# Two-block transformer layer on one core: the upper feed-forward matrices of the second block by seven products of quarters instead of eight

## The chip, the cores and the metric

The kernel runs on one core of a Trainium2 chip. The metric is device time in microseconds (us) of one execution of the whole program, on that core; lower is better. The kernel before took 3178.87 us, the median of three runs (3176.96, 3178.87 and 3190.85).

## The reference, cut to what matters

Two blocks run one after the other on 512 tokens of 1024 features. The first has four sequence mixers and a mixture of 32 experts. The second has two layers of the same shape, and the change is in the feed-forward half of these two:

```python
def hybrid_layer(h, ..., w1, w3, w2, ln2_g, ln2_b, cos, sin):
    ...
    h = layer_norm(ALPHA * h + mix, ln1_g, ln1_b)
    a = jnp.einsum('bld,df->blf', h, w1)
    b = jnp.einsum('bld,df->blf', h, w3)
    y = jnp.einsum('blf,fd->bld', jax.nn.silu(a) * b, w2)
    return layer_norm(ALPHA * h + y, ln2_g, ln2_b)
```

Here `h` has 528 tokens in the first layer (16 of them meta tokens) and 512 that matter in the second; `w1` and `w3` ("upper" matrices) are 1024 x 2816, which is 22 tiles of 128 hidden features each, and `w2` is 2816 x 1024. All is float32.

## The kernel before, in words

**Arithmetic.** A float32 product is made of float32r products. Each operand is cut exactly into a high part `h` (a copy rounded to float32r, on ACT) and a low part `l` (operand minus high part), and three matmuls are summed: high by high, high by low, low by high (`mmf_steps`, L1771 to L1778, with the matmuls on L1775 to L1777). Activations lie feature-major, so the weights are the stationary operand and the tokens the moving one. The tokens go in two halves, of 264 in the first layer and 256 in the second.

**One hidden tile.** A weight tile is a piece of 128 x 1024 (eight blocks of 128 input features). For a hidden tile `f` and a half of the tokens, each of the two matrices takes 8 x 3 matmuls into one PSUM bank. So one hidden tile takes 2 matrices x 2 halves x 24 = 96 matmuls. Then ACT takes the silu of the first product (L2274), Vector multiplies by the second (L2275), and when both halves are there ACT and POOL split the result (L2283, L2284) for the lower product.

**Stages of a layer.** `ffn_ln` (L2255) goes through three parts of the hidden features (`FPARTS`: 8, 8 and 6 tiles). After each part's upper products come the lower products with `w2` (8 output tiles; matmuls on L2297 to L2299), summed into `r`. The first two hidden tiles are treated together: both tiles' first token half, then both tiles' second half, because the second half of `h1` is still being normalised; `rest()` is the end of that norm.

**Weights.** `Split` (L1108) streams all pieces of the second block in order of use through a ring of six slots of 128 x 2048. A slot holds two raw pieces, loaded on SP's queue (512 KB each), or the two parts of one piece, made by ACT (L1141) and Vector (L1142).

**Order.** The program is written stage by stage, and a scheduler then fixes the order on each engine when the program is built; each engine runs its own list strictly in that order. PSUM has eight banks: six for products ("gu" four, "py" two, handed out in turn by `bank`), two for small things.

Of the kernel before, what the change touches and what calls it, by code (L numbers as in the profile page):

```python
# [32 lines left out]
FT = [  # name, columns (-1: zero)  # L33
# [93 lines left out]
def layout(inp):  # L127
    """The inputs laid out for the loads: transposed, cut and padded with zeros."""
# [59 lines left out]
    # experts, in units in the order of use: half, gate or linear, k half; k half, half  # L188
# [10 lines left out]
# ---- second block: 16 meta tokens and 512 tokens, 528 in all  # L199
# [45 lines left out]
def _ret_tables():  # L245
    """rotary tables with the decay gamma^(t - 264) (q) and gamma^(264 - t) / sqrt(dk) (k) folded in"""
# [19 lines left out]
def layout2(inp, o):  # L266
# [57 lines left out]
# ---------------------------------------------------------------- device  # L324
# [30 lines left out]
def softplus_steps(k, pool, z, out):  # L355
    """out = softplus(z) = max(z, 0) + log1p(exp(-|z|))"""
# [17 lines left out]
def block1_mix(k, es_mix):  # L374
    """In-projection and the four mixers. Returns their outputs side by side, feature-major
    [128, 8, 512], in two float32r parts, in a pool of es_mix."""
    nc, tc, A = k.nc, k.tc, k.A
    V, ACT, G, PE = nc.vector, nc.scalar, nc.gpsimd, nc.tensor
    with ExitStack() as es:
# [28 lines left out]
        def wt(shape, name, bufs=1):  # L408
            """working tile; the larger ones share slots by size"""
# [44 lines left out]
        def tproj(name, evac):  # L454
            """one token tile at each step"""
# [24 lines left out]
        def tgate(name):  # L480
            """u * sigmoid(u)"""
# [21 lines left out]
        def conv(name, cw, cb, j, out):  # L503
            """out = silu(causal conv of width 4)"""
# [11 lines left out]
        # ---- row quantities: dt and the cumulated decay (SSD), gates (mLSTM)  # L516
# [75 lines left out]
        # ---- SSD  # L592
        def ssd():
# [61 lines left out]
        # ---- GLA  # L655
        def gla():
# [15 lines left out]
            sc = wt([128, NCH], "gl_sc")     # state: end of chunk c to the middle of c+1  # L672
# [55 lines left out]
        # ---- mLSTM  # L728
        def mlstm():
# [11 lines left out]
            # the gate as tanh(u / 2) = 2 sigmoid(u) - 1  # L741
# [48 lines left out]
        # ---- the mixers' outputs and the weights of the output projection, two float32r parts each  # L790
# [8 lines left out]
        def out_piece(n, i):  # L799
            """two blocks of rows of half n of the columns"""  # L800
# [6 lines left out]
        # ---- RWKV: everything but the recurrence over chunks  # L807
# [97 lines left out]
        def rwkv_chunks():  # L905
# [40 lines left out]
            def bank4(l):  # L946
                """psum for one half of the columns of four heads"""
# [106 lines left out]
# the slots of a block of an expert's tokens, and room for the table of the further blocks  # L1054
# [4 lines left out]
def rsqrt(k, pool, v, out, scale=1.0, eps=0.0):  # L1059
    """out = (v * scale + eps) ** -0.5 for narrow v [p, m]: Newton's iterations from a guess by the exponent"""  # L1060
# [20 lines left out]
def fast_rsqrt(k, pool, v, out, scale=1.0, eps=0.0):  # L1081
    """the same with the tables of logarithm and exponential, where they are loaded"""
# [1423 lines left out]
```

## Time and profile before

| what | value |
|---|---|
| runs | 3176.96, 3178.87, 3190.85 us; median 3178.87 |
| profiled execution | span 3183.1 us from the first to the last instruction; the page gives no other time of it |
| TensorE (PE) busy | 3025.6 us, 95% |
| VectorE (DVE) busy | 2144.0 us, 67% |
| ScalarE (ACT) busy | 1533.5 us, 48% |
| GpSimd (POOL) busy | 819.9 us, 26% |
| mean granted TensorE clock | 0.965 of full speed |

A slice of the span can be bound by another engine than the next slice, so these shares are only a start: the feed-forward stages of the second block are the last third of the span, and have to be read by themselves. "Busy" of PE counts pipelined matmuls, whose recorded lengths overlap; how fast PE goes is read from how many matmuls start in a stretch. An instruction's recorded length also overlaps the next one's start a little on DVE, so the distance between starts tells more than the length.

### The profile page before, as it was taken

To read this page: it belongs to the slowest core of one execution; us is meant where nothing else is said; L and a number is where in the kernel's file an instruction comes from. 1 tells how busy PE (TensorE), PEld (TensorE's weight loads), DVE (VectorE), ACT (ScalarE), POOL (GpSimd) and SP (SyncE) were. 2 spreads that over 40 slices of the span, in tenths; PEclk is the share of its full clock that TensorE was granted. 3 is DMA by queue.
4 is the path that set the end of the run, shared out by engine and by line. 5 is a ranking of instruction groups with operands and counts; after the bars stand their busy time and mean duration, and the time that the engine had idled before them with its cause. 6 is when DMAs were issued, how large, how long until landed. Compare 5 with 4: busy or idle time off the path is not lost. (4 is left out here: it accounts for less than half of the span.)

```text
span 3183.1 us, 45711 instructions
## 1 busy us (share of the span) xinstructions
PE 3025.6 (95%) x18347; PEld 2488.6 (78%) x18347; DVE 2144.0 (67%) x3036; ACT 1533.5 (48%) x1840; POOL 819.9 (26%) x538
## 2 busy tenths in 40 slices
PE   6899879999999999999999899999999899999997
PEld 4799666666666666666666788999999899999997
DVE  4745758999999989799988766653333846834324
ACT  4411426677766666676666644342222534432222
POOL 1210233333333333234322320320102501410104
PEclk8989889999999999999999989999999889999998
DMA  3201268999999999799997121122222211222221
GB/s 121 73 21 41 85 255 319 340 348 350 351 353 340 343 343 334 300 351 344 343 343 244 51 91 41 65 82 91 84 93 80 95 45 50 80 97 90 97 85 52
DMA packets 105991, 581.58 MB, mean 183 GB/s; under 512 B 13016, under 2 KB 13544, under 8 KB 55792
## 3 DMA queue, kind: packets, MB, share of 16 engines
q1 hardware_dynamic: 94784, 540.86, 45.9%
q0 software_dynamic: 10896, 37.52, 4.4%
q8 instruction: 145, 2.38, 0.3%
q14 instruction: 70, 0.57, 0.1%
q10 hardware_dynamic: 96, 0.26, 0.0%
HBM read 559.64 MB, written 18.94 MB: 182 GB/s over the span
## 5 line engine op out<-in xcount | busy, mean ns | idle before, releaser
L1211 DVE TENSOR_TENSOR wl<-w,wh 128x2048 fp32r<-128x2048 f32 (+1 forms) x398 | 909.3, 2293 | 85.0 <-ACT wh L1210 84.0
L1210 ACT ACTIVATE wh<-w 128x2048 fp32r<-128x2048 f32 (+1 forms) x410 | 734.1, 1808 | 133.2 <-PE gu L1150 87.1
L1775 PE MATMUL gu<-hh,w 128*128 128x256 f32 (+2 forms) x1552 | 454.6, 293 | 8.3 <-ACT hh L2473 8.3
L1776 PE MATMUL gu<-hl,w 128*128 128x256 f32 (+2 forms) x1552 | 451.3, 291 | 3.5 <-DVE hl L2475 2.7
L1777 PE MATMUL gu<-hh,w 128*128 128x256 f32 (+2 forms) x1552 | 449.1, 290 | 0.8 <-DVE w L1142 0.8
L1149 PE MATMUL gu<-wl,xT 128*96 128x512 f32 x1024 | 414.6, 405 | 8.8 <-DVE wl L1211 7.4
L1148 PE MATMUL gu<-wh,xT 128*96 128x512 f32 x1024 | 406.1, 397 | 0.2 <-ACT wh L1210 0.2
L1150 PE MATMUL gu<-wh,xT 128*96 128x512 f32 x1024 | 403.9, 394 | 0.0
L1142 DVE TENSOR_TENSOR w<-w 128x1024 fp32r<-128x1024 f32 (+1 forms) x190 | 237.6, 1251 | 234.1 <-ACT w L1141 229.8
L1141 ACT ACTIVATE w<-w 128x1024 fp32r<-128x1024 f32 (+1 forms) x194 | 201.2, 1038 | 259.5 <-PE gu L2299 84.6
L1775 PEld LDWEIGHTS gu<-hh,w 128*128 128x128 f32 x1552 | 300.6, 194 | 11.0 <-ACT hh L2473 9.9
L1776 PEld LDWEIGHTS gu<-hl,w 128*128 128x128 f32 x1552 | 300.0, 193 | 6.6 <-DVE hl L2475 4.4
L1777 PEld LDWEIGHTS gu<-hh,w 128*128 128x128 f32 x1552 | 300.9, 194 | 2.0 <-DVE w L1142 1.3
L1424 POOL TENSOR_TENSOR hg<-hg,sg 96x512 f32<-96x512 f32 x64 | 171.5, 2680 | 333.7 <-ACT sg L1422 333.7
L1149 PEld LDWEIGHTS gu<-wl,xT 128*96 128x96 f32 x1024 | 165.3, 161 | 106.6 <-DVE wl L1211 33.2
L2284 POOL TENSOR_TENSOR al<-fs,ah 128x528 fp32r<-128x528 f32 (+1 forms) x44 | 76.7, 1744 | 608.1 <-ACT ah L2283 608.1
L1148 PEld LDWEIGHTS gu<-wh,xT 128*96 128x96 f32 x1024 | 165.9, 162 | 73.4 <-issue 1.9
L1150 PEld LDWEIGHTS gu<-wh,xT 128*96 128x96 f32 x1024 | 165.8, 162 | 62.6
L1149 PE MATMUL py<-wl,hT 128*96 128x512 f32 x512 | 206.5, 403 | 0.2
L1148 PE MATMUL py<-wh,hT 128*96 128x512 f32 x512 | 204.3, 399 | 0.1
L1150 PE MATMUL py<-wh,hT 128*96 128x512 f32 x512 | 200.9, 397 | 0.0
L1444 POOL DMA_INDIRECT h_d<-y,dx x31 | 119.1, 3840 | 226.2 <-ACT y L1443 222.2
(701 smaller groups left out, 6478.0 us busy)
## 6 DMA issues: line engine op xcount, KB each, us to landing
w<-in_wgu SPq DMA_DIRECT2D x255, 1024.0 KB, 7.3
w<-in_wdn SPq DMA_DIRECT2D x127, 1024.0 KB, 6.5
w<-in_w SPq DMA_DIRECT2D x88, 512.0 KB, 3.5
w<-in_w2f SPq DMA_DIRECT2D x43, 512.0 KB, 3.7
w<-in_w22a SPq DMA_DIRECT2D x32, 512.0 KB, 3.8
w<-in_w1f SPq DMA_DIRECT2D x18, 512.0 KB, 3.5
w<-in_w2o SPq DMA_DIRECT2D x16, 512.0 KB, 3.6
w<-in_w22b SPq DMA_DIRECT2D x16, 384.0 KB, 3.4
```

Source lines behind the costliest of these rows:

```text
L1141: nc.scalar.activation(h, w, AF.Copy)
L1142: (eng or nc.vector).tensor_sub(l, w, h.bitcast(F32))
L1148: PE.matmul(out, a[0], b[0], start=start, stop=False)
L1149: PE.matmul(out, a[0], b[1], start=False, stop=False)
L1150: PE.matmul(out, a[1], b[0], start=False, stop=stop)
L1210: ACT.activation(h[:, j], w[:, j], AF.Copy)
L1211: (early or V).tensor_sub(l[:, j], w[:, j], h[:, j].bitcast(F32))
L1424: G.tensor_mul(hg, hg, sg)
L1444: G.indirect_dma_start(out=h_d, out_offset=bass.IndirectOffsetOnAxis(ap=dx[:, :1], axis=0), in_=y, in_offset=None, compute_op=OP.add)
L1775: PE.matmul(p, w[0][:, kk], x[0][:, kk, c], start=kk == ks[0], stop=False)
L1776: PE.matmul(p, w[0][:, kk], x[1][:, kk, c], start=False, stop=False)
L1777: PE.matmul(p, w[1][:, kk], x[0][:, kk, c], start=False, stop=kk == ks[-1])
```

## The change

Two hidden tiles of one upper matrix and the two halves of the tokens make a product of 2 x 2 quarters: the hidden tiles `f` and `f+1`, the upper and lower four blocks of input features, and the two token halves. Eight products of quarters are needed when written out plainly. The change computes the same with seven (Strassen's algorithm in Winograd's form), each of them 4 blocks x 3 matmuls = 12 into one bank. It needs sums of weight quarters, sums of token quarters, and sums of the seven products:

- `Split.pair` makes seven stationary operands of 128 x 512 from two raw pieces: three subtractions on POOL, one addition on Vector, and seven splits, each a copy on ACT and a subtraction on Vector. The parts fill three slots of the ring and a tile `sp_p` (two buffers).
- `token_sums` makes the four sums of token quarters once per layer, in place in `r`, and splits them.
- `seven` runs the seven products and combines them: one ACT copy and seven Vector additions from PSUM, then `done` for each finished quarter: silu on ACT for `w1`, a multiplication on POOL for `w3`.
- The first two hidden tiles of each layer stay as they were, but one after the other; the other 20 go in ten pairs, for both matrices: 20 pairs of weight tiles per layer, 40 in all.
- Around it: the pieces' order (w1 of both tiles, then w3 of both), buffers of `ah`/`al` (8 for 10), `fs` (4 for 2), the norm's `ln_s`, `ln_T`, `ln_Q` (1 for 2), a bias written back into `r` after the first norm (an ACT instruction for each even tile), the lookahead `AHEAD` set at places, and the last norm's tiles in a pool of their own.

```diff
 class Split:
+    def pair(self, src0, src1, pool):
+        ...
+        w0, w1 = self.raw.pop(0), self.raw.pop(0)
+        a11, a12, a21, a22 = w0[:, 0:512], w0[:, 512:1024], w1[:, 0:512], w1[:, 512:1024]
+        room = []
+        for _ in range(3):
+            t = self.slot(F32R)
+            room += [(t[:, 1024 * i:1024 * i + 512], t[:, 1024 * i + 512:1024 * i + 1024]) for i in range(2)]
+        t = pool.tile([128, 1024], F32R, name="sp_p", bufs=2)
+        room.append((t[:, 0:512], t[:, 512:1024]))
+        t1, t2 = (pool.tile([128, 512], F32, name=n) for n in ("sp_a", "sp_b"))
+
+        def parts(i, x):
+            h, l = room[i]
+            ACT.activation(h, x, AF.Copy)
+            V.tensor_sub(l, x, h.bitcast(F32))
+
+        parts(0, a11)
+        V.tensor_add(t1, a21, a22)
+        G.tensor_sub(t2, t1, a11)
+        parts(1, t2)
+        parts(2, a12)
+        G.tensor_sub(a21, a11, a21)
+        parts(3, a21)
+        parts(4, t1)
+        G.tensor_sub(t2, a12, t2)
+        parts(5, t2)
+        parts(6, a22)
+        return [[x.rearrange("p (a b) -> p a b", a=4) for x in r] for r in room]
...
+    def seven(self, w, h1, T, t0, hn, room, done, bank):
+        def product(i, x, kh, c):
+            p = bank()
+            for kk in range(4):
+                for a, b in ((0, 0), (0, 1), (1, 0)):
+                    PE.matmul(p, w[i][a][:, kk], x[b][:, kh + kk, c], start=kk == a == b == 0, stop=kk == 3 and a == 1)
+            return p
+        ...
+        ACT.activation(r11, product(0, h1, 0, c0), AF.Copy)
+        V.tensor_add(r12, r11, product(1, T[1], 0, ct))
+        V.tensor_add(r11, r11, product(2, h1, 4, c0))
+        done(0, 0)
+        V.tensor_add(r21, r12, product(3, T[2], 0, ct))
+        p = product(4, T[0], 0, ct)
+        V.tensor_add(r22, r21, p)
+        V.tensor_add(r12, r12, p)
+        done(1, 1)
+        V.tensor_add(r12, r12, product(5, h1, 4, c1))
+        done(0, 1)
+        V.tensor_add(r21, r21, product(6, T[3], 0, ct))
+        done(1, 0)
+
+    def token_sums(self, r, pool, hn):
+        ...
+        V.tensor_sub(t[0], b[0][1], b[0][0])
+        G.tensor_sub(t[2], b[1][1], b[0][1])
+        V.tensor_sub(t[1], b[1][1], t[0])
+        V.tensor_sub(t[3], b[1][0], t[1])
+        for i in range(4):
+            ACT.activation(T[i][0], t[i], AF.Copy)
+            V.tensor_sub(T[i][1], t[i], T[i][0].bitcast(F32))
+        return T
...
     def ffn_ln(...):
-                for fs in [(f0, f0 + 1)] * (i == 0) + [(f,) for f in range(f0 + 2 * (i == 0), f1)]:
-                    ws = {(f, nm): self.piece(A[nm][l, f]) for f in fs for nm in ("w21", "w23")}
-                    ...
-                            ACT.activation(ss[f][:, c], pu, AF.Silu)
-                            V.tensor_mul(ss[f][:, c], ss[f][:, c], pg)
+                for f in range(2) if i == 0 else []:
+                    ...
+                        if rest:
+                            rest()
+                            T, rest = self.token_sums(r, tp, hn), None
+                    out(ss)
+                for f in range(f0 + 2 * (i == 0), f1, 2):
+                    s2 = [fs_(), fs_()]
+                    quarter = {(a, b): s2[a][:, half[b]] for a in range(2) for b in range(2)}
+                    def silu(a, b):
+                        ACT.activation(quarter[a, b], quarter[a, b], AF.Silu)
+                    self.seven(sp.pair(A["w21"][l, f], A["w21"][l, f + 1], ff), h1, T, t0, hn, quarter, silu, pt)
+                    tmp = {(a, b): ff.tile([128, hn], F32, name="fg%d%d" % (a, b)) for a in range(2) for b in range(2)}
+                    def times(a, b):
+                        G.tensor_mul(quarter[a, b], quarter[a, b], tmp[a, b])
+                    self.seven(sp.pair(A["w23"][l, f], A["w23"][l, f + 1], ff), h1, T, t0, hn, tmp, times, pt)
+                    for s_ in s2:
+                        out(s_)
```

**Vector in the second part of the first layer.** In the rows below L1142 splits a whole piece before, L1172 a quarter now; L1175 is the weight sum; L2275 is the multiplication before; L2313 to L2323 are the additions of the products from PSUM ("gu" and "py"). `w_19909` is the raw slot of a w3 pair, `w_19912` to `w_19914` and `sp_p_19915` its parts, `fg..` the products of the w3 pair two places ahead of it in the program, `fs_19773` those of the w1 pair between the two. Before, for two hidden tiles:

```order
L2275 TENSOR_TENSOR fs_17921<-fs_17921,gu_17923 128x264
L1142 TENSOR_TENSOR w_18151<-w_18030,w_18151 128x1024
L2275 TENSOR_TENSOR fs_17921<-fs_17921,py_17975 128x264
L1142 TENSOR_TENSOR w_18154<-w_18030,w_18154 128x1024
L2275 TENSOR_TENSOR fs_18039<-fs_18039,gu_18041 128x264
L1142 TENSOR_TENSOR w_18269<-w_18148,w_18269 128x1024
```

Now, for one pair of weight tiles (its last split, of `sp_b`, comes next):

```order
L1172 TENSOR_TENSOR w_19912<-w_19909,w_19912 128x512
L2318 TENSOR_TENSOR fg11_19634<-fg10_19633,gu_19719 128x264
L2319 TENSOR_TENSOR fg01_19632<-fg01_19632,gu_19719 128x264
L1175 TENSOR_TENSOR sp_a_19916<-w_19909 128x512
L2321 TENSOR_TENSOR fg01_19632<-fg01_19632,py_19735 128x264
L1172 TENSOR_TENSOR w_19913<-w_19909,w_19913 128x512
L1172 TENSOR_TENSOR w_19912<-sp_b_19917,w_19912 128x512
L2323 TENSOR_TENSOR fg10_19633<-fg10_19633,gu_19750 128x264
L1172 TENSOR_TENSOR w_19913<-w_19909,w_19913 128x512
L1172 TENSOR_TENSOR sp_p_19915<-w_19909,sp_p_19915 128x512
L1172 TENSOR_TENSOR w_19914<-sp_a_19916,w_19914 128x512
L2313 TENSOR_TENSOR fs_19773<-fs_19773,py_19816 128x264
```

Two splits for two products have become eight instructions on weights among seven additions of products, and the additions of one pair stand behind the splits of the pair after next.

**POOL at the same place.** Before, one low part for each hidden tile:

```order
L2284 TENSOR_TENSOR al_17905<-fs_17646,ah_17904 128x528
L2284 TENSOR_TENSOR al_17909<-fs_17647,ah_17908 128x528
L2284 TENSOR_TENSOR al_18027<-fs_17921,ah_18026 128x528
L2284 TENSOR_TENSOR al_18145<-fs_18039,ah_18144 128x528
L2284 TENSOR_TENSOR al_18263<-fs_18157,ah_18262 128x528
```

Now, for two hidden tiles (L1176, L1179 and L1182 are the weight subtractions, L2392 the multiplications, L2362 the low parts):

```order
L1176 TENSOR_TENSOR sp_b_20057<-sp_a_20056,w_20049 128x512
L1179 TENSOR_TENSOR w_20049<-w_20049 128x512
L1182 TENSOR_TENSOR sp_b_20057<-w_20049,sp_b_20057 128x512
L2392 TENSOR_TENSOR fs_19773<-fs_19773,fg00_19905 128x264
L2392 TENSOR_TENSOR fs_19774<-fs_19774,fg11_19908 128x264
L1176 TENSOR_TENSOR sp_b_20191<-sp_a_20190,w_20183 128x512
L2392 TENSOR_TENSOR fs_19773<-fs_19773,fg01_19906 128x264
L1179 TENSOR_TENSOR w_20183<-w_20183 128x512
L2362 TENSOR_TENSOR al_20040<-fs_19773,ah_20039 128x528
L1182 TENSOR_TENSOR sp_b_20191<-w_20183,sp_b_20191 128x512
L2392 TENSOR_TENSOR fs_19774<-fs_19774,fg10_19907 128x264
L2362 TENSOR_TENSOR al_20044<-fs_19774,ah_20043 128x528
```

Two instructions for two hidden tiles have become twelve, for two pairs of weight tiles.

**PE at the start of the first layer's feed-forward.** Here `w_17631` and `w_17634` are w1 and w3 of hidden tile 0, `w_17640` and `w_17643` those of tile 1 before; `w_17633` and `w_17636` are those of tile 0 now. Before, where the second half of the tokens begins:

```order
L1777 MATMUL gu_17701<-hh_17039,w_17643 128x264
L1775 MATMUL gu_17800<-hh_17039,w_17631 128x264
L1775 MATMUL py_17801<-hh_17039,w_17634 128x264
L1775 MATMUL gu_17852<-hh_17039,w_17640 128x264
L1775 MATMUL gu_17853<-hh_17039,w_17643 128x264
L1776 MATMUL gu_17800<-hl_17040,w_17631 128x264
```

Now, where it begins:

```order
L1819 MATMUL gu_17641<-hh_17039,w_17636 128x264
L1817 MATMUL py_17764<-hh_17039,w_17633 128x264
L1817 MATMUL gu_17765<-hh_17039,w_17636 128x264
L1818 MATMUL py_17764<-hl_17040,w_17633 128x264
L1819 MATMUL py_17764<-hh_17039,w_17633 128x264
```

Tile 1's 48 matmuls with the first half stood ahead of this point before; now only tile 0's do, and tile 1's come later.

## Rows read from the trace of the kernel before

**Rows 1.** The page's busy times: us, share of the span, instructions.
```profile
PE 3025.6 (95%) x18347; PEld 2488.6 (78%) x18347; DVE 2144.0 (67%) x3036; ACT 1533.5 (48%) x1840; POOL 819.9 (26%) x538
```

**Rows 2.** Busy us and counts by window: PE, PEld, DVE, ACT, POOL; clock, DMA, GB/s.
```profile
2270.91:2329.27 58.36, 58.36 (x482) 58.36 (x481) 16.54 (x21) 16.62 (x25) 8.82 (x5) 1.00 0.25 91
2806.19:2862.99 56.80, 56.80 (x482) 56.80 (x481) 16.47 (x20) 16.49 (x25) 9.04 (x5) 1.00 0.26 93
```

**Rows 3.** Time line of DVE, one hidden tile of layer two: start, length, instruction.
```profile
2800.58 0.42 DVE L2275 TENSOR_TENSOR fs<-fs,gu 128x256 f32<-128x256 f32 x1 [3.43 <-PE gu L1777]
2804.71 1.22 DVE L1142 TENSOR_TENSOR w<-w 128x1024 fp32r<-128x1024 f32 x1 [3.71 <-ACT w L1141]
...
2807.33 1.23 DVE L1142 TENSOR_TENSOR w<-w 128x1024 fp32r<-128x1024 f32 x1 [0.72 <-ACT w L1141]
2811.94 0.42 DVE L2275 TENSOR_TENSOR fs<-fs,gu 128x256 f32<-128x256 f32 x1 [3.38 <-PE gu L1777]
```

**Rows 4.** Time line of DVE, instructions back to back while POOL is idle.
```profile
2740.72 0.68 DVE L2442 TENSOR_TENSOR ln_Q<-ln_Q,ln_sq 128x512 f32<-128x512 f32 x1
2741.33 0.68 DVE L2240 SCALAR_TENSOR_TENSOR r<-hl,r 128x512 f32<-128x512 f32 x1
2741.93 0.41 DVE L2430 TENSOR_TENSOR r<-r,gu 128x256 f32<-128x256 f32 x1
2742.26 1.21 DVE L1142 TENSOR_TENSOR w<-w 128x1024 fp32r<-128x1024 f32 x1
```

**Rows 5.** Groups by line: count, busy us, mean ns of one, idle before.
```profile
L1210 ACT ACTIVATE wh<-w 128x512 fp32r<-128x512 f32 x12 | 6.6, 619 | 0.5 <-PE gu L1150 0.5
...
L2284 POOL TENSOR_TENSOR al<-fs,ah 128x528 fp32r<-128x528 f32 x22 | 38.6, 1755 | 308.9 <-ACT ah L2283 308.9
...
L2478 POOL TENSOR_TENSOR r<-r,ln_T 128x264 f32<-128x264 f32 x16 | 15.1, 970 | 9.2 <-ACT ln_T L2455 9.2
```

**Rows 6.** Time lines of POOL and DVE where both work, at three places.
```profile
2496.91 3.54 POOL L2477 TENSOR_TENSOR r<-r,ln_mean 128x264 f32<-128x264 f32 x4 [4.48 <-ACT ln_mean L2451]
...
2496.68 0.48 DVE L2471 SCALAR_TENSOR_TENSOR r<-ln_mrs,cp,r 128x264 f32<-128x264 f32 x1
2497.08 0.97 DVE L2475 SCALAR_TENSOR_TENSOR hl<-r,cp,hh 128x264 fp32r<-128x264 f32 x1
2497.97 0.97 DVE L2470 SCALAR_TENSOR_TENSOR r<-r,cp,ln_T 128x264 f32<-128x264 f32 x1
...
2730.93 3.44 POOL L2426 TENSOR_TENSOR r<-r,ln_s 128x512 f32<-128x512 f32 x2 [1.74 <-issue]
...
2733.14 1.78 DVE L2240 SCALAR_TENSOR_TENSOR r<-hl,r 128x512 f32<-128x512 f32 x1
...
2487.92 4.12 POOL L2478 TENSOR_TENSOR r<-r,ln_T 128x264 f32<-128x264 f32 x4 [0.77 <-ACT ln_T L2455]
...
2490.45 0.41 DVE L2430 TENSOR_TENSOR r<-r,py 128x264 f32<-128x264 f32 x1
```

**Rows 7.** Landing times of the loads on L1126 (SP).
```profile
DMA to landing us min/median/max: 2.9/3.6/5.9
```

**Rows 8.** Start of layer one's feed-forward: windows as in rows 2, PE, DVE.
```profile
2095.00:2101.00 6.00, 4.11 (x34) 3.90 (x32) 4.11 (x7) 4.65 (x7) 3.52 (x4) 1.00 0.44 165
2101.00:2107.00 6.00, 4.70 (x25) 4.48 (x26) 5.42 (x14) 4.40 (x11) 0.09 (x1) 0.72 0.01 3
...
2101.22 0.39 PE L1775 MATMUL gu<-hh,w 128*128 128x264 f32 x1 [2.10 <-ACT hh L2473]
...
2097.36 0.43 DVE L2456 SCALAR_TENSOR_TENSOR ln_mrs<-ln_mean,ln_T 128x264 f32<-128x264 f32 x1 [1.89 <-ACT ln_T L2455]
...
2106.23 0.42 DVE L1684 TENSOR_TENSOR hl<-r,hh 128x264 fp32r<-128x264 f32 x1
```

More of the change, by code (lines that the diff above doesn't have):

```diff
@@ L1143, in __call__ @@
         return h, l
+    def pair(self, src0, src1, pool):
+        nc = self.k.nc
+        V, ACT, G = nc.vector, nc.scalar, nc.gpsimd
+        for i, src in enumerate((src0, src1)):
+            want = self.srcs[self.n + i]
+            assert (want.tensor.name, want.offset, want.shape) == (src.tensor.name, src.offset, src.shape)
+        while self.loaded < self.n + 2:
+            self.load()
+        self.n += 2
+        w0, w1 = self.raw.pop(0), self.raw.pop(0)
[23 more added lines that the diff above has]
+        return [[x.rearrange("p (a b) -> p a b", a=4) for x in r] for r in room]
 def mm3(PE, out, a, b, start, stop):
@@ L1714, in run @@
                     hp = ExitStack()
-                    last = l == k.n_layers - 1
-                    h = None if last else self.new_h(hp, "right")
-                    self.ffn_ln(l, h1, h, t0, LayerNorm(self, lp, r, T2 - t0, "ln2", l, t0), rest)
+                    new = None if l == k.n_layers - 1 else lambda: self.new_h(hp, "right")
+                    h = self.ffn_ln(l, h1, new, t0, LayerNorm(self, lp, r, T2 - t0, "ln2", l, t0), rest)
                 h1p.close()
@@ L1729, in pieces @@
         for i, (f0, f1) in enumerate(FPARTS):
-            for f in range(f0, f1):
-                yield A["w21"][l, f]
-                yield A["w23"][l, f]
+            for f in range(f0, f1, 2):
+                for j in ((f, "w21"), (f, "w23"), (f + 1, "w21"), (f + 1, "w23")) if f == 0 else \
+                        ((f, "w21"), (f + 1, "w21"), (f, "w23"), (f + 1, "w23")):
+                    yield A[j[1]][l, j[0]]
             for m in range(8):
@@ L2253, in proj_ln, with ffn_ln @@
         return self.late(3, tile, mm, ln, h1)
-    def ffn_ln(self, l, h1, hn_, t0, ln, rest):
+    def seven(self, w, h1, T, t0, hn, room, done, bank):
+        PE, V, ACT = self.nc.tensor, self.nc.vector, self.nc.scalar
+        def product(i, x, kh, c):
[4 more added lines that the diff above has]
+            return p
+        c0, c1, ct = slice(t0, t0 + hn), slice(t0 + hn, t0 + 2 * hn), slice(0, hn)
+        r11, r12, r21, r22 = (room[ab] for ab in ((0, 0), (0, 1), (1, 0), (1, 1)))
+        ACT.activation(r11, product(0, h1, 0, c0), AF.Copy)
[12 more added lines that the diff above has]
+    def token_sums(self, r, pool, hn):
+        nc = self.nc
+        V, ACT, G = nc.vector, nc.scalar, nc.gpsimd
+        b = [[r[:, 4 * i:4 * i + 4, hn * j:hn * j + hn] for j in range(2)] for i in range(2)]
+        T = [[pool.tile([128, 4, hn], F32R, name="T%d%d" % (i, j)) for j in range(2)] for i in range(4)]
+        t = [b[0][0], b[1][1], b[0][1], b[1][0]]
+        V.tensor_sub(t[0], b[0][1], b[0][0])
[6 more added lines that the diff above has]
+        return T
+    def ffn_ln(self, l, h1, new, t0, ln, rest):
         nc, A, sp = self.nc, self.A, self.sp
@@ L2261, in ffn_ln, with out @@
         r, pt = ln.r, ln.bank
+        half = [slice(0, hn), slice(hn, n)]
         with tile_pool(self.tc, name="ff", bufs=1) as ff:
+            es_t = ExitStack()
+            tp = es_t.enter_context(tile_pool(self.tc, name="ts", bufs=1, side="right"))
             for i, (f0, f1) in enumerate(FPARTS):
                 act = []
[L2265 to L2275 removed]
+                def out(s_):
+                    a = (ff.tile([128, n], F32R, name="ah", tag="ah", bufs=8),
+                         ff.tile([128, n], F32R, name="al", tag="al", bufs=8))
+                    ACT.activation(a[0], s_, AF.Copy)
+                    G.tensor_sub(a[1], s_, a[0].bitcast(F32))
+                    act.append(a)
+                fs_ = lambda: ff.tile([128, n], F32, name="fs", bufs=4)
+                for f in range(2) if i == 0 else []:
+                    sp.AHEAD = 2 - f
+                    ws = {nm: self.piece(A[nm][l, f]) for nm in ("w21", "w23")}
+                    ss = fs_()
+                    for q in range(2):
+                        pu, pg = pt(), pt()
+                        for nm, p in (("w21", pu), ("w23", pg)):
+                            self.mmf(p, ws[nm], h1, range(8), slice(t0 + hn * q, t0 + hn * q + hn))
+                        ACT.activation(ss[:, half[q]], pu, AF.Silu)
+                        V.tensor_mul(ss[:, half[q]], ss[:, half[q]], pg)
                         if rest:
@@ L2278, in ffn_ln @@
                             self.dump_h("h1_%d" % l, h1, ff, t0)
-                            rest = None
-                    for f in fs:
-                        a = (ff.tile([128, n], F32R, name="ah", tag="ah", bufs=10),
-                             ff.tile([128, n], F32R, name="al", tag="al", bufs=10))
-                        ACT.activation(a[0], ss[f], AF.Copy)
-                        G.tensor_sub(a[1], ss[f], a[0].bitcast(F32))
-                        act.append(a)
+                            T, rest = self.token_sums(r, tp, hn), None
[12 more added lines that the diff above has]
+                        out(s_)
+                if i == 2:
+                    es_t.close()
+                    hn_ = new and new()
+                sp.AHEAD = 2
                 def tile(m):
@@ L2301, in ffn_ln @@
                 for m in range(8 - 3 if i == 2 else 8):
+                    if m == 6 and i < 2:
+                        sp.AHEAD = 1
                     w, p = tile(m), (pt(), pt())
@@ L2313, in ffn_ln @@
             if hn_ is None:
-                self.finish(3, tile, mm, ln, ff)
+                with tile_pool(self.tc, name="fin", bufs=1, side="right") as fin:
+                    self.finish(3, tile, mm, ln, fin)
             else:
@@ L2400, in __init__ @@
         self.nm, self.l, self.t0, self.st, self.turn = nm, l, t0, {}, 0
[L2401 removed]
+        t = lambda nm: pool.tile([128, n], F32, name=nm)
         self.s, self.T, self.Q = t("ln_s"), t("ln_T"), t("ln_Q")
@@ L2475, in apply @@
                     V.scalar_tensor_tensor(dst[1][d], x, b, y.bitcast(F32), op0=OP.add, op1=OP.subtract)
+                    if nm == "ln1":
+                        ACT.activation(x, x, AF.Identity, bias=b)
             else:
```

8 lines of the change are left out of this document (1 added, 7 removed).

## The prediction

> **What bounds the kernel now.** I read the busy times first, then windows of the stage that changes, then Vector's and POOL's time lines inside it. Over the whole span PE is busy 95% and POOL 26% [rows 1], but that is a mean over many stages. In the upper products of the second block the windows are clearer: in a stretch of five hidden tiles PE is busy all 58.36 us in the first layer and all 56.80 us in the second, at full clock, while Vector works some 16.5 us of it and POOL 9 [rows 2]. The reader should see two things. First, PE waits for nothing here: five tiles are 480 matmuls, so one takes 121.6 ns in the first layer (264 tokens) and 118.3 ns in the second (256); fewer matmuls would be time saved one for one, as long as the others keep up. Second, the others have much room: in a hidden tile of 11.36 us Vector runs two splits of 1.2 us and two short multiplications and waits the rest [rows 3].
>
> **What is removed.** A pair of weight tiles took 2 tiles x 2 halves x 24 = 96 matmuls and now takes 7 x 12 = 84. There are 20 pairs per layer. Saved: 20 x 12 x 0.1216 = 29.2 us in the first layer, 20 x 12 x 0.1183 = 28.4 in the second, **57.6 us** in all. PE's time for a pair falls from 11.67 to 10.21 us (first layer) and from 11.36 to 9.94 (second). The change cannot give more than this, since nothing else is taken from PE.
>
> **What is added, engine by engine, for one pair of weight tiles.**
>
> ACT: seven copies of 512 at 0.62 us [rows 5], one copy from PSUM and on average two silus and one high part, some 0.4 to 0.6 us each: about 6 us of 10. It hides beside PE. If it didn't, PE would wait for weights, but the margin is 4 us.
>
> Vector: seven splits and one sum of 512 elements, each with two operands in SBUF, 0.60 us from start to start when POOL is idle, and seven additions from PSUM, 0.33 us for 256 columns, taken as 0.34 [rows 4]. That is 8 x 0.60 + 7 x 0.34 = 7.2 us of 10.2. By itself it hides.
>
> POOL: three subtractions of 512, on average two multiplications of 264 and one low part of 528. At 1.7, 0.97 and 1.76 us [rows 5] (the row for 528 scaled to 512) this is 8.8 us, where a tile had one instruction of 1.76. It hides too, but barely.
>
> **Where the two collide.** The rows that matter show POOL and Vector at once [rows 6]. POOL runs four instructions of 264 in 3.54 us, and Vector's instructions with two SBUF operands then take 0.97 us each and start 0.89 apart; the one just ahead of them took 0.48, so each is lengthened by 0.49. One of 512 takes 1.78 in place of the 0.68 of rows 4, 1.10 more. But an addition that reads PSUM keeps its 0.41 us in the middle of POOL's work. So each POOL instruction can hold up one two-operand Vector instruction: by 1.10 us if it has 512 elements, 0.49 for 264, about 1.13 for 528. [...]
>
> POOL's holds for one pair are 3 x 1.10 + 2 x 0.49 + 1.13 = 5.4 us. If none of it delays Vector, Vector needs 7.2 us a pair; if all does, 12.6, more than PE's 10.2. The additions (2.4 us) are the only Vector work that can run under a hold. I take half of them as placed so, 1.2 us, since splits and additions are mixed in the order and neither engine waits for the other on purpose: 7.2 + 5.4 - 1.2 = **11.4 us**. Then it is Vector that sets the pace of a pair, and lags by 11.4 - 10.21 = 1.19 us a pair in the first layer and 1.46 in the second. What is late next are the banks: a product's bank comes free only with its addition, which is queued behind the splits of the pair after next, and PE can run six products ahead.
>
> How much lag is free? The raw pieces of the pair after next take the ring slot that the third and fourth products leave, at 4 x 12 x 0.1216 = 5.8 us from the pair's start. They land 3.6 us later [rows 7], ACT copies (0.6), Vector splits (0.6): 10.6. Behind that stand three additions, the weight sum and two splits (2.8) with about two holds (2.2), then the seventh product's addition: 15.9 us. Its bank is wanted by the sixth product of the next pair, at 10.2 + 7.3 = 17.5. So about 1.6 us of lag cost nothing, anew in each of the three parts of a layer, because between the parts the lower products let Vector catch up. There the first two pairs of parts two and three are also split ahead, and the first pair of the layer is split before its products, so 15 of 20 pairs per layer cost Vector in full. PE's waits: 15 x (1.19 + 1.46) = 39.8, less 6 x 1.6 = 9.6: **30.2 us** given back. The ends for this term are 0 (no hold bites) and 15 x (2.39 + 2.66) - 9.6 = 66 (every hold bites).
>
> **The start of each layer.** Before, PE fills the time in which the second half of the first norm is finished with tile 1's first half, and still waits 2.1 us at 2101.22; then it runs at a clock of 0.72 in the stretch behind [rows 8]. Now these 48 matmuls, 5.8 us, come after the wait. Besides, one sum of 1056 elements, one split of 1056 and one of 512 stand ahead of the last low part of the norm on Vector, whose run there lasts from 2097.36 to 2106.2; at 1.2 us (the row of 1024 in rows 4) twice and 0.6 they delay it by 3.0 us. As tile 1's matmuls can fill part of that, I count 1.2. So 7.0 us a layer, **14 us** in all (ends: 5.7 and 8.8 a layer). The rest of the token sums, five more such instructions on Vector, runs beside tile 1's 11.7 us on PE. The added biases on ACT and the changed buffers I count at nothing: ACT is less than two thirds busy there, and each smaller set of buffers is used again only after the lower products, in PE's own order.
>
> **Sum.** -57.6 + 30.2 + 14 = -13.4 us against the span of 3183.1. The median of the runs shown is 4.2 us below that span, so I apply the difference to the median: 3178.9 - 13.4 = **3165.5**, said as 3165. A measurement of this kernel can tell about 0.5%, 16 us, from no change, so this lies just inside.
>
> **The rivals.**
>
> *The holds fall where they don't hurt.* If POOL works mostly under additions and waits for PE, Vector stays under 10 us a pair and only the start costs: -57.6 + 2 x 5.7 = -46, about 3133. For it: Vector had 70% of its time free before [rows 2]. Against it: POOL's 8.8 us of work leave little time in which it is idle. Chance 0.2.
>
> *Every hold costs in full.* Vector's additions come in runs, the splits in others, and POOL's subtractions are needed just when Vector splits. Then a pair takes Vector 12.6 us and the term is 66, with 8.8 us a layer at the start: -57.6 + 66 + 17.6 = +26, about 3205. It becomes slower than before when a pair takes Vector longer than 11.9 us or so, where the waits pass 43.6 (57.6 less 14): (43.6 + 9.6) / 30 = 1.77 above the mean of PE's 10.21 and 9.94. [...] For it in the rows: the starts 0.89 apart, again and again, where both engines had work [rows 6]. Against it: the additions keep their length. Chance 0.25.
>
> *The loads come late.* A pair now has one load window instead of several, since its slot frees only with the fourth product. If loads land in 5.9 us (the slowest in rows 7) and not 3.6, the free lag of 1.6 is gone and 0.7 us more is lost on each of 30 pairs: -13.4 + 9.6 + 21 = +17, about 3196. Chance 0.1; it needs the slowest load every time.
>
> That the change doesn't do what it says I leave out: the order on PE has 480 matmuls fewer, 40 pairs x 12.
>
> **How the numbers follow.** My forecast has 0.45. Its own range, with a pair on Vector between 10.9 and 11.9 us (30 x 0.5 us either way), is 3150 to 3180. Faster by over 0.5% (below 3163): the first rival, 0.2, and half of the forecast, 0.22, so 0.42. Within 0.5%: the other half and the milder parts of the two slow rivals, 0.36. Slower by over 0.5% (above 3195): 0.22. The range of 8 in 10 reaches from the first rival to the second, 3135 to 3207.
>
> **What the profile after would show.** PE's windows in the upper products: under 100% busy, with waits for Vector's additions (banks) or for L1172's low parts. Vector's L1172 of 512: a mean well above 0.68, near 1.1 to 1.3, and L2313 to L2323 near 0.43. POOL busy over two thirds of such a window. Successive L2313 of one layer some 11 us apart late in a part, near 10.2 early in it. At the layer's start a PE wait of some 8 us for the norm. I am wrong if L1172 stays at 0.68 (then the first rival), if PE mostly waits for DMA or for ACT, or if the first pairs of a part are as slow as the last, which would take the free lag away.

## The result, and the profile after the change

The changed kernel takes 3240.98 us (median of 4 runs, 3234.58 to 3243.35), the kernel before 3182.96 on the same chip: a ratio of 1.0176, with a 95% interval of 1.0154 to 1.0199. It is slower by 58 us, outside the predicted range (3135 to 3207) on the slow side. The profiled span rose from 3183.1 to 3239.0, by 55.9. Since 57.6 us of matmuls are gone, 113.5 us were given back, where 44.2 were forecast.

The busy times of the page, against [rows 1]:

```profile
PE 3009.7 (93%) x17867; PEld 2459.4 (76%) x17867; DVE 2446.3 (76%) x3490; ACT 1640.5 (51%) x2103; POOL 1066.9 (33%) x740
```

The loss is found by windows that begin and end with a stage. Of the kernel before: the first part's lower products and the second part's upper products in layer 1, then the same two in layer 2 (columns as in [rows 2]).

```profile
2185.80:2233.95 48.15, 47.26 (x386) 47.04 (x385) 23.17 (x39) 9.03 (x9) 1.81 (x1) 1.00 0.24 88
2233.95:2327.33 93.38, 93.38 (x770) 93.38 (x769) 26.91 (x33) 26.06 (x39) 12.49 (x7) 1.00 0.25 91
...
2862.79:2910.02 47.23, 46.33 (x386) 46.13 (x385) 22.92 (x39) 9.00 (x9) 1.78 (x1) 1.00 0.30 106
2910.02:3000.91 90.89, 90.89 (x770) 90.89 (x769) 26.77 (x33) 25.86 (x39) 12.32 (x7) 1.00 0.24 85
```

The same four stages after the change:

```profile
2202.83:2253.87 51.04, 49.20 (x386) 48.55 (x385) 29.94 (x48) 11.65 (x16) 12.76 (x10) 0.97 0.18 63
2253.87:2353.46 99.59, 88.70 (x675) 87.04 (x674) 78.94 (x113) 42.74 (x80) 48.25 (x39) 0.95 0.26 96
...
2904.00:2957.01 53.01, 49.41 (x386) 48.42 (x385) 28.90 (x50) 10.23 (x14) 10.60 (x9) 0.94 0.23 80
2957.01:3048.42 91.41, 83.67 (x674) 82.41 (x673) 76.81 (x112) 42.72 (x82) 51.95 (x40) 0.96 0.26 93
```

In the second part PE has 96 matmuls fewer, 11.7 us in layer 1, and yet the stage is 6.2 us longer: PE idles 10.9 us of 99.59, and its mean clock is 0.95 where it was 1.00. The lower products, whose matmuls the change leaves alone, are 2.9 and 5.8 us longer. Done for all stages (length after, less length before, plus the matmuls removed there), this gives the table; in a layer's first part the pairs are counted from their first product on, 78.65 and 73.40 us against 504 matmuls at 0.1216 and 0.1183, and the rest of that stage is the start:

| given back, us | forecast | measured |
|---|---|---|
| pairs, six parts | 30.2 | 79 (17.4, 17.9, 10.7; 13.8, 11.9, 7.5) |
| start of the two layers | 14 | 14 (7.7 and 6.3) |
| lower products, six parts (the third parts with what follows them) | 0 | 22 |

The stages add up to some 115; the rest of the program, some 2 us shorter, makes up the difference to 113.5. So two terms failed, and the size of the start did not.

What PE waits for in the second block (in total, times, longest):

```profile
PE gu L2307 <- ACT fs L2312: 22.6, 10, 4.0
PE py L1817 <- ACT hh L2592: 12.1, 2, 7.0
PE gu L2307 <- DVE fs L2313: 11.4, 4, 3.9
PE py L2307 <- DVE fs L2313: 7.8, 2, 3.9
PE py L2412 <- ACT ah L2361: 6.7, 6, 1.8
...
PE py L2413 <- POOL al L2362: 4.7, 6, 1.0
```

L2312 and L2313 are the instructions that free the banks of products 0 and 1; L1817's waits are for the norm at the start of a layer, and L2412 and L2413 are matmuls of the lower products. Ten of the waits for a bank are 3.2 to 4.0 us long; they come from about the middle of a part on, once for every two pairs of weight tiles. One cycle of two pairs, late in part two of layer 1, as a window:

```profile
2313.70:2341.13 27.43, 22.95 (x168) 22.22 (x168) 22.30 (x32) 11.28 (x22) 15.41 (x12) 0.94 0.31 116
```

PE's 168 matmuls are 20.5 us at a clock of 1.00 (0.122 us each). Vector works 22.30 us, 11.15 a pair (10.5 in the same place of layer 2), where 11.4 was forecast: the holds, by which a POOL instruction lengthens one of Vector's, have about the size that was read from [rows 6] (the largest group of L1172 has a mean of 1.12 us where 0.68 is the free length, and the additions keep their 0.42). But the cycle lasts 27.43, and Vector idles 5 us of it. Its end on PE, ACT, DVE and POOL:

```profile
2341.60 0.39 PE L2307 MATMUL gu<-hh,w 128*128 128x264 f32 x1 [3.88 <-DVE fs L2313]
...
2338.64 0.64 ACT L2361 ACTIVATE ah<-fs 128x528 fp32r<-128x528 f32 x1 [2.71 <-POOL fs L2392]
2339.19 0.61 ACT L1171 ACTIVATE w<-sp_a 128x512 fp32r<-128x512 f32 x1
...
2333.24 0.42 DVE L2323 TENSOR_TENSOR fg<-fg,py 128x264 f32<-128x264 f32 x1
2335.16 1.13 DVE L1172 TENSOR_TENSOR w<-w 128x512 fp32r<-128x512 f32 x1 [1.50 <-ACT w L1171]
...
2339.90 1.30 DVE L1172 TENSOR_TENSOR w<-sp_a,w 128x512 fp32r<-128x512 f32 x1 [1.90 <-ACT w L1171]
2341.13 0.42 DVE L2313 TENSOR_TENSOR fs<-fs,gu 128x264 f32<-128x264 f32 x1
...
2334.42 1.32 POOL L2362 TENSOR_TENSOR al<-fs,ah 128x528 fp32r<-128x528 f32 x1
2335.70 1.76 POOL L1182 TENSOR_TENSOR sp_b<-w,sp_b 128x512 f32<-128x512 f32 x1
2337.42 1.18 POOL L2392 TENSOR_TENSOR fs<-fs,fg 128x264 f32<-128x264 f32 x1
```

Read it from the bottom. The last gate multiplication (L2392) of the finished pairs stands in POOL's order behind a low part and a weight subtraction of the next ones: its last input is there at 2333.66, when L2323 ends, and it starts 3.76 us later. ACT's high part (L2361) waits for it, 2.71 us, and behind it on ACT stands a copy of the next weights (L1171). Vector's low part of these weights (L1172) waits for that, and behind it stands L2313, for which PE waits 3.88 us. Over the cycle no engine is full (POOL works 15.41 us of it, though without a pause in the 8.3 us up to the end of L2392); four orders are coupled. In layer 2 the same chain ends with L2312, which stands right behind L2361 on ACT. POOL's records differ too: its L1182, of 512 elements, which began while Vector's split of 2335.16 was running, is recorded with 1.76 us, and L2362, of 528, which began beside an idle Vector, with 1.32.

What a stall costs besides, as two windows behind that stall:

```profile
2342.30:2345.70 3.40, 3.40 (x18) 3.40 (x17) 2.62 (x6) 2.11 (x4) 0.00 (x0) 0.51 0.00 0
2346.00:2349.40 3.40, 3.40 (x30) 3.40 (x29) 2.11 (x5) 1.80 (x4) 0.00 (x0) 1.00 0.00 0
```

PE has work, but at a clock of 0.51 it starts 18 matmuls where it then starts 30: 12 x 0.122 = 1.5 us more. The same is seen at nine of the ten long stalls: 3.4 us or more at a clock of 0.50 to 0.53, which begin within 1 us of the stall's end. It is not seen at the one of 3.3 us that ends at 2866.07 (1.00 in the 11.9 us behind it). The two waits of 0.9 us at the start of the lower products of part two in layer 1 are followed by it as well (18 matmuls at 0.50 from 2359.40 on). Taking (1 - clock) x length over all upper and lower stages after the first pair of a layer, I estimate that at most 31 us of the loss are clock; before, these stages ran at 1.00.

### The profile page after: what moved, and what is told of

Its sections match the earlier page's. It is cut to its first block, busy times and chain, and to the rows that moved or that the text cites. A ratio compares the mean times of both kernels' runs of the same rounds, so it can differ in the third digit from the quotient of the medians.

```text
span 3239.0 us, 45978 instructions
## 1 busy us (share of the span) xinstructions
PE 3009.7 (93%) x17867; PEld 2459.4 (76%) x17867; DVE 2446.3 (76%) x3490; ACT 1640.5 (51%) x2103; POOL 1066.9 (33%) x740
## 5 line engine op out<-in xcount | busy, mean ns | idle before, releaser
L1817 PE MATMUL gu<-hh,w 128*128 128x256 f32 (+2 forms) x688 | 211.5, 308 | 6.1 <-ACT hh L2592 6.1
L1818 PE MATMUL gu<-hl,w 128*128 128x256 f32 (+2 forms) x688 | 208.1, 303 | 3.0 <-DVE hl L2594 2.4
L1819 PE MATMUL gu<-hh,w 128*128 128x256 f32 (+2 forms) x688 | 205.6, 299 | 0.8 <-DVE w L1142 0.8
L1142 DVE TENSOR_TENSOR w<-w 128x1024 fp32r<-128x1024 f32 (+1 forms) x110 | 141.9, 1291 | 53.0 <-ACT w L1141 52.3
L1141 ACT ACTIVATE w<-w 128x1024 fp32r<-128x1024 f32 (+1 forms) x114 | 116.3, 1023 | 118.3 <-PE gu L2414 57.8
L1439 POOL DMA_INDIRECT xg<-x_d,ix x32 | 78.7, 2460 | 261.4 <-issue 186.9
L1172 DVE TENSOR_TENSOR w<-w 128x512 fp32r<-128x512 f32 x120 | 132.2, 1117 | 24.0 <-ACT w L1171 22.9
L2307 PE MATMUL gu<-hh,w 128*128 128x264 f32 (+1 forms) x640 | 132.1, 289 | 17.2 <-DVE fs L2313 11.4
L1817 PEld LDWEIGHTS gu<-hh,w 128*128 128x128 f32 x688 | 138.7, 202 | 8.4 <-ACT hh L2592 7.3
```

Source lines behind the costliest of these rows:

```text
L1142: (eng or nc.vector).tensor_sub(l, w, h.bitcast(F32))
L1172: V.tensor_sub(l, x, h.bitcast(F32))
L1817: PE.matmul(p, w[0][:, kk], x[0][:, kk, c], start=kk == ks[0], stop=False)
L1818: PE.matmul(p, w[0][:, kk], x[1][:, kk, c], start=False, stop=False)
L1819: PE.matmul(p, w[1][:, kk], x[0][:, kk, c], start=False, stop=kk == ks[-1])
L2307: PE.matmul(p, w[i][a][:, kk], x[b][:, kh + kk, c], start=kk == a == b == 0, stop=kk == 3 and a == 1)
```

## The experiments

Theory A: the order of the queues makes the long stalls. Theory B: Vector's pace under POOL's holds, by which I had forecast, makes them. Theory C: the loads are late. The kernel before takes 3181.33 to 3182.96 us beside all runs here, so times of different sets are compared directly.

**High parts behind the next weights** (POOL and Vector keep their work; `last` is the copy of part 5):

```
-                    self.seven(sp.pair(A["w23"][l, f], A["w23"][l, f + 1], ff), h1, T, t0, hn, tmp, times, pt)
-                    for s_ in s2:
-                        out(s_)
+                    ws = sp.pair(A["w23"][l, f], A["w23"][l, f + 1], ff)
+                    with self.tc.issue_after(sp.last.ins): [out(s_) for s_ in held]
+                    self.seven(ws, h1, T, t0, hn, tmp, times, pt)
+                    held = s2
+                for s_ in held: out(s_)
```

> The changed kernel, but ACT's two high parts of a finished pair of tiles (L2361) stand in ACT's order behind the copies of the next pair's weights, not between them; POOL's low parts (L2362) follow. PE's order is the same. In the changed kernel two products of weights (168 matmuls, 20.5 us of PE in layer 1) take 27.43 us from stall to stall, with one stall of 4.0 us and Vector busy 22.3 us of it. Theory A (the order of the queues: L2361 waits for POOL's last multiplication, which stands behind weight subtractions of 1.7 us, and holds up the weight copies behind it on ACT, so Vector's L1172 and the L2313 that frees a bank): the ten stalls of 3.3 to 4.2 us in the upper products go, a cycle falls to Vector's own 22.3 us, ten cycles x 5 us less, so the span falls from 3239 to about 3190 (3180 to 3200). Theory B (Vector's pace under POOL's holds is what counts, and its waits only follow from PE): a cycle stays above 26 us and the span within 12 us of 3239. Theory C (loads late): the same as B, with ACT's waits for the loads in place of those for L2392.

Measured: 3212.89 us, ratio to before 1.0091 (1.0058 to 1.0123), span 3215.4. Part two's upper products in layers 1 and 2:

```profile
2249.74:2342.55 92.81, 84.70 (x675) 82.63 (x673) 76.57 (x111) 42.30 (x80) 46.64 (x37) 1.00 0.26 97
...
2944.44:3027.88 83.44, 80.77 (x674) 79.73 (x673) 78.99 (x111) 41.73 (x82) 53.21 (x40) 1.00 0.29 101
```

The long stalls are gone (the longest wait for a bank is 1.8 us) and the clock is back at 1.00 in these products. PE's and Vector's orders in the second block are the same as in the changed kernel, instruction by instruction; only some places on ACT and POOL differ. So the order made the long stalls. In layer 2 Vector is now busy 78.99 of 83.44 us: with the chain cut, the pace there is Vector's, as forecast. The six parts give back 42 us in place of 79. The gain is smaller than theory A expected, 28 us and not 49. A cycle falls to 23.0 us in layer 2 but only to 26.0 in layer 1, where theory A had 22.3: Vector still idles there behind ACT's copies, which wait for POOL's sums (5.1 and 2.2 us in one cycle). And the lower products get longer (53.6 us in part two of layer 1 for 51.1), since the high parts now come later at a part's end. So theory A names the cause of the long stalls but not the size of the gain; theory B's span, within 12 us of 3239, is missed too.

**Weight subtractions on Vector** (everything else as changed), and **both edits**:

```
-        G.tensor_sub(t2, t1, a11)
+        V.tensor_sub(t2, t1, a11)
...
-        G.tensor_sub(a21, a11, a21)
+        V.tensor_sub(a21, a11, a21)
...
-        G.tensor_sub(t2, a12, t2)
+        V.tensor_sub(t2, a12, t2)
```

> The changed kernel, but the three weight subtractions of a pair (L1176, L1179, L1182) run on Vector and not on POOL. By its rows Vector's own work for a pair rises from 8 to 11 two-operand instructions at 0.60 us and 7 additions at 0.34: 9.0 us, and POOL's holds fall to 2 x 0.49 + 1.13 = 2.1, so 9.0 to 11.1 us a pair, 18 to 22.2 a cycle of two. Theory A (order of the queues): POOL's last multiplication no longer stands behind weight subtractions, so L2361 comes some 4 us earlier and holds nothing up; a cycle falls from 27.43 to 21 or 22 us, the span to about 3180 (3165 to 3195). Theory B (Vector's pace alone): Vector's busy time falls by at most 1.1 us of 22.3 a cycle, and the span by some 10 to 20 us, to 3220 to 3230. If the additional work on Vector outweighs the holds, the span rises above 3239.

> Both edits at once: the high parts behind the next weights on ACT, and the weight subtractions on Vector. Theory A: with either edit the chain is broken, so the second adds only what it saves Vector, at most 1 us a cycle: within 15 us of the better of the two alone, about 3175. If the two give the sum of their gains, there were two causes and not one.

Measured: 3180.59 us for the first, ratio 1.0003 (0.9982 to 1.0023); 3164.05 for both, ratio 0.9942 (0.9920 to 0.9964). Part two's upper products in layer 1, of the first and then of both:

```profile
2226.96:2311.22 84.26, 82.89 (x674) 82.26 (x673) 74.97 (x127) 42.00 (x80) 22.18 (x19) 1.00 0.29 101
```

```profile
2237.76:2319.88 82.12, 82.12 (x674) 82.12 (x673) 72.67 (x130) 42.33 (x80) 21.03 (x19) 1.00 0.30 108
```

Vector has three instructions more a pair and with both edits is busy for less time, 72.67 us in place of 78.94, and PE waits for nothing there: of the 11.7 us of removed matmuls 11.3 are gained in that stage. The single edit gained 60 us, which is theory A's number; the second 17 more, where theory A allowed 15 and the sum of the two alone would be 88. The runs of these two kernels spread over 17 and 22 us, so the times don't tell 16.5 from 15. In the stage shown the two edits alone take 6.8 and 15.3 us off the 99.59, and 17.5 together: they overlap. The single edit can't say by itself what it cured, since it does three things: it takes weight subtractions from ahead of the multiplication in POOL's queue, it takes their holds from Vector, and with it the scheduler also places other instructions differently on Vector and ACT. What the holds do alone is the next run.

**POOL's load without its results**: the kernel with both edits, and POOL does three subtractions a pair besides that nobody reads (`self.dump` is a tile of the next norm that is idle then).

```
-        V.tensor_sub(t2, t1, a11)
+        V.tensor_sub(t2, t1, a11); G.tensor_sub(self.dump, t1, a11)
...
-        V.tensor_sub(a21, a11, a21)
+        V.tensor_sub(a21, a11, a21); G.tensor_sub(self.dump, a12, a22)
...
-        V.tensor_sub(t2, a12, t2)
+        V.tensor_sub(t2, a12, t2); G.tensor_sub(self.dump, a12, a22)
```

> The kernel with both edits (high parts behind the next weights, weight subtractions on Vector; 3164 us), and POOL makes three subtractions of 512 elements a pair besides, at the same places, whose results nobody reads: POOL's load of before without its results being waited for. Theory D1 (POOL's holds on Vector are what the subtractions cost): by rows 4 to 6 of the prediction a pair takes Vector 9.0 us of its own, 2.1 of holds that are there already and up to 3 x 1.10 more: 12 to 14 us, over PE's 10.2, so a cycle goes from 20.5 to 24 to 27 us and the time to 3215 or more. Theory D2 (the way of each sum over POOL to ACT and back to Vector is what they cost): nobody waits for these, so the time stays within 12 us of 3164.

Measured: 3266.91 us, ratio 1.0283 (1.0249 to 1.0317), 103 us over the kernel without them. Vector and ACT run the same instructions in the same order in both. Part two's upper products in layer 2 and Vector's first subtraction of weights, without POOL's load and with it:

```profile
2909.78:2989.09 79.31, 79.31 (x674) 79.31 (x673) 74.78 (x134) 43.21 (x82) 23.65 (x20) 1.00 0.30 107
...
L1176 DVE TENSOR_TENSOR sp_b<-sp_a,w 128x512 f32<-128x512 f32 x39 | 26.6, 682 | 0.0
```

```profile
2964.45:3062.61 98.16, 86.69 (x675) 84.44 (x673) 95.44 (x133) 42.45 (x82) 55.53 (x40) 0.95 0.24 87
...
L1176 DVE TENSOR_TENSOR sp_b<-sp_a,w 128x512 f32<-128x512 f32 x38 | 61.5, 1618 | 0.0
```

Vector is busy 95.44 of 98.16 us: it is the pace, and it hardly waits. Without the added load it was busy 74.78 us in this stage, so three subtractions on POOL lengthen its work by 20.66 / 8 = 2.6 us a pair; 3.3 had been counted before the overlap with additions. This is the hold by itself (1618 ns in place of 682 for the subtraction shown), and theory D1 stands. Whether the way of a sum over POOL to ACT and back costs something besides in the changed kernel, no run shows.

**Gate multiplications on Vector** (everything else as changed):

```
-                        G.tensor_mul(quarter[a, b], quarter[a, b], tmp[a, b])
+                        V.tensor_mul(quarter[a, b], quarter[a, b], tmp[a, b])
```

> The changed kernel, but the gate multiplications (L2392) run on Vector; POOL keeps the weight subtractions and the low parts. Vector gets 4 instructions of 264 at about 0.40 us a cycle of two pairs, and loses the holds of POOL's four. Theory A (order of the queues): L2361 on ACT no longer waits for POOL, so the chain is cut a third way; the ten stalls of 3.3 to 4.2 us go, a cycle is 23 to 24 us as with the high parts moved back (26.0 in layer 1, 23.0 in layer 2 there), and the lower products start sooner besides: span 3239 to about 3195 (3185 to 3205). Theory D (what counts are POOL's weight subtractions, through their holds on Vector and their place between ACT's copies; moving them gained 60 us where moving the high parts gained 28): less than 15 us, above 3225.

Measured: 3214.0 us, ratio 1.0107 (1.0076 to 1.0138). Neither number was right: 27 us gained, between the two. The chain is cut and the longest wait for a bank falls to 1.9 us, but PE now waits for additions on Vector, which in layer 2 is busy 84.88 of part two's 88.42 us:

```profile
PE gu L2307 <- DVE fs L2314: 12.0, 7, 1.9
PE py L2307 <- DVE fs L2314: 7.6, 4, 1.9
```

**The start as before** (both tiles' first halves ahead of the rest of the norm; the body of the loops over `q` and `f` is the same):

```
-                for f in range(2) if i == 0 else []:
...
-                    for q in range(2):
+                    for q, f in ((0, 0), (0, 1), (1, 0), (1, 1)):
...
-                        if rest:
+                        if rest and f:
```

> The changed kernel, but tiles 0 and 1 of each layer are done as in the kernel before: both tiles' first halves of the tokens before the second half of the norm is wanted. Predicted cost of the changed start: 7.0 us a layer, 14 in all. In the trace of the changed kernel the wait for the norm is 7.0 us in layer 1 and 5.3 in layer 2, against 2.1 and 2 before. If those waits are the start's cost: the first PE wait there falls to 2 or 3 us, and the span by 8 to 15 us, to 3224 to 3231. If the norm's end is what is late (sums of tokens ahead of it on Vector), the wait only moves behind the 48 matmuls, and the span falls by less than 4 us. The stalls late in the parts stay in either case.

Measured: 3232.01 us, ratio 1.0147 (1.0099 to 1.0194), an interval that overlaps that of the changed kernel; the four runs lie between 3222.48 and 3240.54, so the time alone does not decide. The profiled execution is one of the longer ones; the spans are 3238.6 and 3239.0. From the last projection before the norm to the first lower product, layer 1 takes 125.85 us (129.41 as changed) and layer 2 119.60 (119.29). The wait for the norm is 2.29 us, and another takes its place, for the low parts of the token sums on Vector:

```profile
2104.65 0.39 PE L1817 MATMUL gu<-hh,w 128*128 128x264 f32 x1 [2.29 <-ACT hh L2592]
...
2122.89 1.61 PE L2307 MATMUL gu<-T,w 128*128 128x264 f32 x11 [2.83 <-DVE T L2341]
```

So, by these traces, the order of two tiles on PE is worth 3.6 us of the 7.7 in layer 1 and nothing in layer 2. For the rest the trace names Vector's list of sums; no run takes that list away, so this is read and not shown.

**The end of a part on Vector**: both edits, and the last pair's multiplications and low parts on Vector; then the same with the start as before. With both edits alone the lower products of part two take 54.01 and 52.76 us, against 48.01 and 47.23 in the kernel before; PE idles 3.8 and 3.2 us of it, and its mean clock is 0.94.

```
-                        G.tensor_mul(quarter[a, b], quarter[a, b], tmp[a, b])
+                        (V if f == f1 - 2 else G).tensor_mul(quarter[a, b], quarter[a, b], tmp[a, b])
...
-                for s_ in held: out(s_)
+                for s_ in held: out(s_, V)
```

> The kernel with both edits (3164 us), and for the last pair of each part the gate multiplications and the low parts run on Vector and not on POOL. [...] If POOL's two slow steps at the end of the chain are the cause (0.75 to 1.2 and 1.3 to 1.76 us, against 0.41 to 0.48 and 0.68 on Vector), a part's lower products fall to 49 or 50 us, 4 us x 6: the time to 3140 (3132 to 3148). If the splits of the lower products' weights, which stand in Vector's order there, are what is late, less than 8 us.

> The same, with the start of the layer as in the kernel before (both tiles' first halves ahead of the norm's second half). That edit alone took 3.6 us from the start of layer 1 and nothing from layer 2's, since the sums of tokens on Vector were late in its place; so within 8 us of the kernel without it. If it now takes 10 us or more, the sums were late there only because POOL's weight subtractions held Vector up.

Measured: 3145.54 us, ratio 0.9895 (0.9868 to 0.9922), inside the expected 3132 to 3148; with the start as before 3142.0, ratio 0.9878 (0.9834 to 0.9922), which is the same. The lower products of part two, both layers, with both edits alone and then in the first of these:

```profile
2319.88:2373.89 54.01, 50.23 (x387) 49.29 (x386) 25.15 (x43) 11.64 (x16) 5.67 (x5) 0.94 0.19 72
...
2989.09:3041.85 52.76, 49.57 (x386) 48.67 (x385) 21.73 (x37) 10.22 (x14) 5.38 (x5) 0.94 0.23 81
```

```profile
2304.76:2353.28 48.52, 47.49 (x387) 47.09 (x385) 26.99 (x46) 11.64 (x16) 0.00 (x0) 1.00 0.21 77
...
2962.52:3009.93 47.41, 46.50 (x387) 46.19 (x386) 24.33 (x43) 10.23 (x14) 0.00 (x0) 1.00 0.25 90
```

They are back near the 48.0 and 47.2 us of the kernel before, at a clock of 1.00. Those of part one are not (51.0 and 52.4 us, before 48.2 and 47.2): PE still waits 1.0 to 2.1 us there for the high part; what makes up the rest of the difference is not shown. Both versions beat both kernels: by 1.0% and 1.2% the kernel before, by 3% the changed one.

Theory C had no run of its own, but the trace of the changed kernel speaks against it: in the upper products of parts two and three no engine waits for a load once the part is 11 us old, and the long stalls there come later. In the first part of layer 1 the last such wait ends at 2151.08, before the first long stall, which ends at 2160.78; in that of layer 2 there is none. And with both edits PE's upper products in part two run without a wait, with the same loads.

## Why the prediction was wrong

**The matmuls saved: right.** With the waits away, part two's upper products take 82.12 us in layer 1 where they took 93.38: 11.3 us less, forecast 11.7.

**The start of a layer: right in size, not in its cause** (7.7 and 6.3 us, forecast 7.0). I had put 5.8 of the 7.0 down to tile 1's matmuls, which now come behind the wait for the norm (7.0 and 5.1 us). With these put back, 3.6 us were gained in one layer and nothing in the other, so that the number came out is in part luck.

**Vector's time for a pair: nearly right** (11.15 us in layer 1 and 10.5 in layer 2, forecast 11.4), and so is its cause, the holds: in the run with POOL's load alone, 2.6 us a pair for the weight subtractions.

**The step that failed is the one from Vector's time to PE's waits.** I let Vector work without a pause, lag by 1.2 to 1.5 us a pair, and gave away 1.6 us of lag in each part; ACT I dismissed with "about 6 us of 10. It hides beside PE", POOL with "It hides too, but barely". These are sums of durations. What decides is what stands behind a waiting instruction: ACT is busy 11 us of 27 and yet holds up Vector, because its L2361 waits for POOL's L2392 with the next weights' copies behind it. That chain made the long stalls; they went with each of three edits that cut it, and one of these changed nothing but the order. With it cut by order alone, 42 us are given back by the pairs and not 79, nearer to my 30 and inside its ends of 0 and 66: 37 us are the chain's, with the clock that its stalls cost. What the other 12 us over my 30 are is not shown; in layer 1 Vector still idles there behind copies that wait for POOL.

**Two costs were not in the sum at all.** The clock: at all but one of the long stalls a stretch of 3.4 us or more at a clock of 0.50 to 0.53 begins, by my estimate at most 31 us lost in all together with the lower products' share. I had such a stretch in front of me at the layer's start (0.72 in [rows 8]) and did not carry it over to the stalls I forecast. And the end of a part: the last pair's multiplication and low part are on POOL, in series with a high part on ACT, and the lower products wait for them; I counted the lower products as time in which Vector catches up, with no cost of their own. They cost 22 us with what follows them; with the end of a part on Vector, those of part two cost 0.5 and 0.2, those of part one still 2.9 and 5.2.

The second rival (every hold costs in full, 3205) had the right direction and, by the run with POOL's load alone, a measured effect behind it (1618 ns where 682 is the free length), but is not what happened either: Vector's time stayed at 11.15 us and did not reach 12.6. The list of what would prove me wrong held: "if PE mostly waits for ... ACT" was met, and the waits for L2312 lead the list.

## What to carry to other kernels

When a step is spread over three in-order engines, draw for each queue what stands behind the instruction that waits longest; a sum of durations per engine finds the floor, not the time. Work for the next piece should not stand behind the finish of the last one in any queue, and the end of a stage deserves the quickest engine for its last two steps (on Vector and not on POOL, 48.52 us for the lower products of part two in layer 1 in place of 54.01). Before a short operation with two SBUF inputs goes to POOL to spare Vector, count what it does to Vector's own: here Vector did eleven of them in less time than eight with POOL's help (74.97 us for 78.94 in part two of layer 1, by the weight subtractions alone).

## What was not expected of the hardware

With both edits Vector had three instructions more a pair and was busy 8% less (72.67 us for 78.94), and POOL's subtractions whose results nobody reads cost 103 us. In the upper products of the changed kernel stalls of 1.4 to 1.8 us left the clock at 1.00, while at one of 1.9 us, at nine of the ten long ones, and at two of 0.9 us close together in the lower products, 3.4 us or more at a clock of 0.50 to 0.53 began; at one stall of 3.3 us the clock stayed at 1.00.
